# Branch product: three direct k tiles, four pairs by blocks, five direct, all sums on VectorE; MLP operand sums on VectorE; the bias of w2 added at its first accumulators

## The chip, the cores and the metric

The kernel runs on one core of a Trainium2 chip. The metric is the device time of one launch in microseconds, taken as the median of several runs.

## What is computed

One layer over 1024 latent tokens (x, width 1024) and 256 context tokens: two token mixers side by side (a Mamba-2 SSD branch and a gated linear recurrence), a gated merge, an output projection, and a squared-ReLU MLP. Everything is float32. Cut to what the change touches:

```
u      = gated_rmsnorm(y_ssd, z, ssd_norm_w)               # 1024 x 2048
br_ssd = u @ w_br_ssd                                      # 2048 x 1024: "the branch product"
x_mix  = (g_ssd * br_ssd + g_lru * br_lru) @ w_out
x      = layer_norm(alpha * x + mx[2] * x_mix, ln1_g, ln1_b)
h2     = layer_norm(x) * (1 + mx[4]) + mx[3]
mlp    = square(relu(h2 @ w_mlp1 + b_mlp1)) @ w_mlp2 + b_mlp2
out    = layer_norm(alpha * x + mx[5] * mlp, ln2_g, ln2_b)
```

## The kernel before

Every float32 operand is split into a high part (ScalarE copy, `A.activation(hi, raw, AF.Copy)`) and a low part (VectorE subtract), and every product is three matmuls on TensorE: high by high, high by low, low by high (`mm3`). A matmul here is 128 x 128 by 128 x 512.

**The branch product** has 16 k tiles of 128. Before, `wino` does them in two chunks of four pairs, by blocks in the manner of Strassen and Winograd: instead of eight block products there are seven (n = 1, 5, 6, 7, 2, 4, 3), each of 4 pairs x 4 output tiles x 3 matmuls = 48, so 2 x 7 x 48 = 672 matmuls, named `wp`. The operands of a block product are sums of input tiles (line L615: names `k0`, `k1`, `s1`), and the outputs are sums of products (L618, L659: name `ba`). `on=None` puts most of those sums on GpSimd (G, shown as POOL); the first sums of the first chunk, two of the output combinations and the additions of the second chunk run on VectorE (V, shown as DVE), which also makes every low part (`oll`, `orl`, L611). The inputs of u are scaled by a row of reciprocal norms (`rb`, loaded by a broadcast DMA) in a VectorE instruction (L710) of 128 x 1024.

**The merge** (`acc<-k,wh`) with the LRU branch and the **output projection** (`op`, L937 to L939) follow. For each of eight token tiles VectorE adds the projection to x (L940), normalises it (L132 to L826), and ScalarE makes `xn` (L821), which TensorE transposes (`tp`, L918). On the first token tile VectorE also scales the row of w2's bias by the gate (`rbmlp<-rbmlp,rmx`, L945, behind the DMA `rmx<-drow`), and GpSimd adds that row to each of the eight token tiles (L946) before the tile is stored.

**The first MLP product** works by blocks too, with operands T1 to T4 and B22 formed from the blocks of h2. The upper blocks are kept only as high and low parts, so GpSimd adds those up again (L974, L985, L986) and makes another difference (L987); VectorE makes L981, L983 and the low parts (L840). `others` issues the products in the order T2, T1, T4, T3, B22. The weight sums for each group are made by `prep` on GpSimd (L891 to L897).

**The second MLP product** (w2) already has the form that the branch gets now: direct k tiles in front, whose 16 output tiles ScalarE copies out of PSUM (L1111), four pairs by blocks per chunk with all sums on VectorE, and direct tiles behind.

All DMAs are issued by SP's queue in one order, and an instruction that waits holds up all behind it on its engine. The order on each engine comes from a scheduler that follows program order, priorities (`tc.high_priority`) and the reuse of pool buffers.

Of the kernel before, what the change touches and what calls it, by code (L numbers as in the profile page):

```python
# [60 lines left out]
def tile_hybrid_layer(ctx: ExitStack, tc: tile.TileContext, x, xc, wmod, win, wdt, lruw, wbs, wbl,  # L61
# [528 lines left out]
    def wino(kts, chunks, raw0, raw1, opr, load_l, load_r, accs, preset, fin, hook, add5, von=(), on=None, bank=0):  # L590
# [4 lines left out]
        for q, ch in enumerate(chunks):  # L595
# [50 lines left out]
            for ni, n in enumerate((1, 5, 6, 7, 2, 4, 3)):  # L646
# [8 lines left out]
                for i in range(4):  # L655
# [10 lines left out]
                    elif n == 7:  # L666
                        comb(3, a[7][i], a[7][i], a[6][i], OP.add)
                        comb(4, a[6][i], a[6][i], a[5][i], OP.add)
                        comb(5, a[5][i], fin5[i], a[7][i], OP.add)
                        fin(1, 1, i, a[5][i])  # L670
# [3 lines left out]
                if hook and last and n in (7, 3):  # L674
                    hook(n)

# [5 lines left out]
    kb0 = bx.enter_context(tc.tile_pool(name="kb0", bufs=8, side="right", reuse_waits="tile"))  # L682
    ac = bx.enter_context(tc.tile_pool(name="bac", bufs=12, side="right", reuse_waits="tile"))
    ox = ExitStack()
    kb1 = ox.enter_context(tc.tile_pool(name="kb1", bufs=2, side="right", reuse_waits="tile"))
# [5 lines left out]

    def braw1():
        n1[0] += 1
        if n1[0] % 8 in (1, 2):
            return kb1.tile([128, 1024], F32, name="k1", bufs=2)
        return wp.tile([128, 1024], F32, tag={3: "wr", 4: "wr", 5: "wh", 6: "wl", 7: "wh", 0: "wl"}[n1[0] % 8], name="k1", bufs=2)

    def load_bw(k, t_):
        Q.dma_start(t_, wbs[k])
        return t_  # L700
# [3 lines left out]
    def load_u(t, t_):  # L704
# [4 lines left out]
        Q.dma_start(t_, du[t])  # L709
        V.scalar_tensor_tensor(t_, t_, vec("normw", t), rbs[g], op0=OP.mult, op1=OP.mult)  # L710
        return t_

    accs = [[mhA.tile([128, 512], F32, tag={2: "mhh", 4: "mhh", 1: "mhl", 6: "mhl"}[n], name="ba", bufs=8) if n in (1, 6, 2, 4) else
             ac.tile([128, 512], F32, name="ba", bufs=12) for i in range(4)] for n in (1, 5, 6, 7, 2, 4, 3)]
# [29 lines left out]
    for th in range(2):  # L744
        sl = slice(th * 512, th * 512 + 512)
        yt = []
        with tc.high_priority(offset=100):
            for k in range(KT):
                raw = evp.tile([128, 512], F32, tag="ev", name="yraw")
                Q.dma_start(raw, dyl[k][:, sl])  # L750
                t_ = braw0().bitcast(F32R)
# [46 lines left out]
    b2r = brow(cp, "bmlp2")  # L798
# [122 lines left out]

    toks = []
    for th in range(2):
        tok = []
        for i in range(4):
# [37 lines left out]
    w0 = prep(0, None)  # L963
# [4 lines left out]
    rws = [cp.tile([128, 2, 512], F32, tag="r" + n_, name="rw", bufs=1) for n_ in ("ln1g", "ln1b", "bmlp2")]  # L968
    r12, r21, r22 = [], [], []
    sums = []  # L970
    b2t = wp.tile([128, 2, 512], F32, tag="wr", bufs=2, name="b2t")
    for k in range(KH):
        sums.append(tt.tile([128, 512], F32, name="b1", bufs=KH))
        G.tensor_tensor(sums[k], B11[k][0].bitcast(F32), B11[k][1].bitcast(F32), op=OP.add)  # L974
    with tc.high_priority(offset=2000):
        for k in range(KH):
# [8 lines left out]
            G.tensor_tensor(b11, B21[k][0].bitcast(F32), b11, op=OP.subtract)  # L985
            G.tensor_tensor(b11, b11, B21[k][1].bitcast(F32), op=OP.add)  # L986
            G.tensor_tensor(b12, b22, b12, op=OP.subtract)  # L987
            r12.append(b12)
            r21.append(b11)
            r22.append(b22)  # L990
        for dst, src in ((T4, r21), (T3, r12), (B22, r22)):
            for k in range(KH):
                split_to(dst[k], ALL, src[k])
# [102 lines left out]
    def direct(ops, i, n_, tag="acc", bufs=4):  # L1096
        pt = ps.tile([128, 512], F32, tag=tag, bufs=bufs, name="mo")
        ts_ = slice(i % 4 * 128, i % 4 * 128 + 128)
        for j, (la, rb) in enumerate(ops):
            mm3(pt, la[i // 4][0][:, ts_], la[i // 4][1][:, ts_], rb[n_][0], rb[n_][1], j == 0, j == len(ops) - 1)  # L1100
        return pt

    with tc.high_priority(offset=60):
        front = [halves(m, of_mha) for m in FRONT[:2]]
        front += [whole(m, raw1) for m in FRONT[2:]]
    pre = {}
# [100 lines left out]
```

## Time and profile before

| | |
|---|---|
| three runs | 2434.9, 2440.69, 2438.38 us, median 2438.38 |
| profiled run | 2443.13 us |
| its span, first to last instruction | 2441.3 us |
| TensorE busy | 96% |
| VectorE, ScalarE, GpSimd busy | 77%, 46%, 17% |
| mean granted clock of TensorE | 0.987 |

The profiled run is one execution. Matmuls are pipelined, so what TensorE loses is read from the starts of its matmuls and from how many of them lie in a stretch.

### The profile page before, as it was taken

Reading aid. Unit: us, or ns where it says so; the run is one execution under the profiler, and the core shown is the slowest. Engines: PE = TensorE matmul, PEld = TensorE weight load, DVE = VectorE, ACT = ScalarE, POOL = GpSimd, SP = SyncE. Lnnn points to the kernel's source line nnn. Section 1 sums busy time; section 2 is a strip of 40 time slices with the busy share of each in tenths; the row PEclk is TensorE's granted clock in tenths of the full one; section 3 lists DMA queues with packets and bytes.
Section 4 is the critical chain, followed back from the end, with each engine's and each line's share of the span. In section 5 each row is a group of like instructions: output and inputs, shape, how many; then the busy total and the mean of one; then the engine's idle time right before and its main releaser. Section 6 shows DMA issues by size and latency. Waiting matters only on the chain. (4 is left out here: it accounts for less than half of the span.)

```text
span 2441.3 us, 31541 instructions
## 1 busy us (share of the span) xinstructions
PE 2353.7 (96%) x11437; PEld 1877.2 (77%) x11437; DVE 1889.2 (77%) x3170; ACT 1112.5 (46%) x1947; POOL 418.3 (17%) x357
## 2 busy tenths in 40 slices
PE   7999999999999999999999998899979999999998
PEld 3877888787877878787787886577757888888876
DVE  6986688678888887888886579977687555638998
ACT  3766856544344354434434363232255554545421
POOL 1000000001011010101111346501365322000004
PEclk9999999999999999999999999999989999999999
DMA  9422144323334253433325640367225333614132
GB/s 345 133 65 66 57 163 154 97 77 105 87 96 112 70 139 77 114 87 96 105 78 142 229 156 26 106 219 244 87 73 164 112 114 100 257 70 149 59 112 87
DMA packets 131636, 294.73 MB, mean 121 GB/s; under 512 B 14596, under 2 KB 47492, under 8 KB 131352
## 3 DMA queue, kind: packets, MB, share of 16 engines
q1 hardware_dynamic: 131480, 292.71, 37.7%
q8 instruction: 90, 1.47, 0.3%
q14 instruction: 66, 0.54, 0.1%
HBM read 243.83 MB, written 53.03 MB: 122 GB/s over the span
## 5 line engine op out<-in xcount | busy, mean ns | idle before, releaser
L114 PE MATMUL acc<-hl,wh 128*128 128x512 f32 (+1 forms) x1560 | 595.9, 382 | 0.6 <-DVE hl L182 0.6
L115 PE MATMUL acc<-hh,wl 128*128 128x512 f32 (+1 forms) x1560 | 593.8, 381 | 0.0
L113 PE MATMUL acc<-hh,wh 128*128 128x512 f32 (+1 forms) x1560 | 591.0, 379 | 2.2 <-ACT hh L177 2.2
L114 PEld LDWEIGHTS acc<-hl,wh 128*128 128x128 f32 x1560 | 295.3, 189 | 58.1 <-issue 12.9
L113 PEld LDWEIGHTS acc<-hh,wh 128*128 128x128 f32 x1560 | 295.1, 189 | 51.8 <-issue 3.1
L115 PEld LDWEIGHTS acc<-hh,wl 128*128 128x128 f32 x1560 | 295.2, 189 | 47.8 <-issue 4.5
L544 POOL TENSOR_SCALAR_AFFINE_SELECT R<-R 128x512 f32<-128x512 f32 x128 | 93.4, 753 | 1114.8 <-DMA R<-dcum 1094.3
L114 PE MATMUL wp<-orl,olh 128*128 128x512 f32 x504 | 201.0, 399 | 23.7 <-DVE orl L611 23.7
L549 ACT ACTIVATE L<-R,cumT 128x128 f32<-128x128 f32 x512 | 163.5, 390 | 126.4 <-issue 58.1
L102 ACT ACTIVATE wh<-wr 128x1024 fp32r<-128x1024 f32 x113 | 119.4, 1057 | 221.4 <-PE acc L114 157.5
L115 PE MATMUL wp<-orh,oll 128*128 128x512 f32 x504 | 198.3, 393 | 0.0
L113 PE MATMUL wp<-orh,olh 128*128 128x512 f32 x504 | 195.6, 393 | 0.3 <-DVE ba L659 0.2
L103 DVE TENSOR_TENSOR wl<-wr,wh 128x1024 fp32r<-128x1024 f32 x113 | 140.3, 1242 | 28.7 <-ACT wh L102 26.7
L114 PEld LDWEIGHTS wp<-orl,olh 128*128 128x128 f32 x504 | 95.5, 189 | 52.3 <-DVE orl L611 32.7
L527 DVE SCALAR_TENSOR_TENSOR H<-H,dec,misc 128x64 f32<-128x64 f32 x512 | 104.9, 274 | 24.1 <-PE misc L519 23.1
L97 POOL TENSOR_TENSOR mv<-mv,mhalf 128x1 f32<-128x1 f32 x34 | 30.5, 898 | 526.1 <-DVE mv L96 524.3
L610 ACT ACTIVATE olh<-k 128x512 fp32r<-128x512 f32 x108 | 67.9, 629 | 109.1 <-PE wp L114 107.2
L113 PEld LDWEIGHTS wp<-orh,olh 128*128 128x128 f32 x504 | 95.7, 190 | 21.6 <-DVE ba L659 0.6
L115 PEld LDWEIGHTS wp<-orh,oll 128*128 128x128 f32 x504 | 95.9, 190 | 19.3
L611 DVE TENSOR_TENSOR oll<-k,olh 128x512 fp32r<-128x512 f32 x108 | 88.0, 815 | 28.2 <-ACT olh L610 27.9
L611 DVE TENSOR_TENSOR orl<-k,orh 128x512 fp32r<-128x512 f32 x126 | 104.5, 830 | 1.6 <-ACT orh L610 1.6
L888 DVE TENSOR_TENSOR xl<-wr,xh 128x512 fp32r<-128x512 f32 x75 | 74.7, 1000 | 32.2 <-ACT xh L887 31.9
(325 smaller groups left out, 4982.0 us busy)
## 6 DMA issues: line engine op xcount, KB each, us to landing
wr<-in_win_dram SPq DMA_DIRECT2D x80, 512.0 KB, 3.6
R<-dcum SPq DMA_DIRECT2D x64, 512.0 KB, 5.2
wr<-in_w_dram SPq DMA_DIRECT2D x37, 512.0 KB, 3.8
wm<-in_wmod_dram SPq DMA_DIRECT2D x32, 512.0 KB, 3.7
E<-decum SPq DMA_DIRECT2D x64, 256.0 KB, 4.5
da<-r SPq DMA_DIRECT2D x64, 256.0 KB, 2.8
k<-da SPq DMA_DIRECT2D x26, 512.0 KB, 5.7
k<-in_w_dram SPq DMA_DIRECT2D x20, 512.0 KB, 4.7
```

What stands on the lines that cost most here:

```text
L97: G.tensor_tensor(dst, dst, mhalf[:, :n], op=OP.pow)
L102: A.activation(hi, src, AF.Copy)
L103: V.tensor_tensor(lo, src, hi.bitcast(F32), op=OP.subtract)
L113: P.matmul(pt, wh, mh, start=first, stop=False)
L114: P.matmul(pt, wh, ml, start=False, stop=False)
L115: P.matmul(pt, wl, mh, start=False, stop=last)
L527: V.scalar_tensor_tensor(H[:, k, d_, hs_2], H[:, k - 1, d_, hs_2], dec[:, k, d_ * 32 + 2 * t + h:d_ * 32 + 2 * t + h + 1], sp[:, k - k0, d ...
L544: G.affine_select(out=rv, in_=rv, compare_op=OP.is_ge, fill=-BIG, base=0, pattern=[[0, 2], [0, 2], [sg, 128]], channel_multiplier=-sg)
L549: A.activation(L[:, q], R[:, q, (p % 2) * 128:(p % 2 + 1) * 128], AF.Exp, bias=ncumT[:, p, col:col + 1])
L610: A.activation(hi, src, AF.Copy)
L611: V.tensor_tensor(lo, src, hi.bitcast(F32), op=OP.subtract)
L888: V.tensor_tensor(ts[i][1], v, ts[i][0].bitcast(F32), op=OP.subtract)
```

## The change

- Branch product: k tiles 0 to 2 go directly (`direct`: 16 output tiles x 3 tiles x 3 matmuls = 144 matmuls, copied out of PSUM by ScalarE), tiles 3 to 10 as four pairs by blocks (336 matmuls, all sums on VectorE), tiles 11 and 12 directly (96 matmuls), tiles 13 to 15 directly (144). The output tiles of the direct parts behind are added by VectorE (L786 after). Together 720 matmuls.
- `rb` has one buffer in place of two.
- The blocks of h2 are also written to DRAM (`dh2`, eight stores) and read back (`b1`, `b21`, eight loads); the sums of the T operands and the first `prep` run on VectorE. `others` takes T1, T2, T3, T4, B22 with T4 formed from a reloaded tile.
- L945, the DMA `rmx` and the eight L946 are gone. The bias of w2 is loaded into the buffer of `ln2g` and added by VectorE at the evacuation of w2's front tiles; `ln2g` itself is loaded again later.

```diff
-    wino([c_ * 8 + k + h_ for c_ in range(2) for k in range(4) for h_ in (0, 4)], [4, 4], braw0, braw1, bop,
-         load_bw, load_u, accs, (), bfin, None, None, (2,3))
+    with tc.high_priority(offset=HP0):
+        front = [parts(t, of_kbf, in_ac, 2, 1) for t in range(3)]
+    pre = {}
+    for r_, c_ in ((0, 0), (1, 0), (0, 1), (1, 1)):
+        pre[r_, c_] = [ac.tile([128, 512], F32, name="ba", bufs=16) for i in range(4)]
+        for i in range(4):
+            A.activation(pre[r_, c_][i], direct(front, r_ * 4 + i, c_), AF.Copy)
+    def bhook(n):
+        if n == 6:
+            btail[0] = [parts(t, of_kbf, in_evp, 2, 1) for t in range(11, 13)]
+        elif n == 3:
+            btail[1] = [parts(13, of_kbf, braw0, 1, 1)] + [parts(t, of_bop, braw0, 1, 2) for t in range(14, 16)]
+    wino([k + h_ for k in range(3, 7) for h_ in (0, 4)], [4], braw0, braw1, bop,
+         load_bw, load_u, accs, (2, 3, 4), bfin, bhook, badd5, on=V, bank=1)
+    for q in range(2):
+        for c_ in range(2):
+            for i in range(8):
+                pt = direct(btail[q], i, c_, *(("acc", 4), ("y", 3))[q])
+                V.tensor_tensor(ys[i][c_], ys[i][c_], pt, op=OP.add)
...
-            rbs[g] = kb1.tile([128, 1024], F32, name="rb", bufs=2)
+            rbs[g] = kbf.tile([128, 1024], F32, name="rb", bufs=1)
...
-            if th == 0 and i == 0:
-                V.scalar_tensor_tensor(b2r, b2r, 1.0 / ALPHA, brow(cp, "mx5", "x1", NX), op0=OP.mult, op1=OP.mult)
-            G.tensor_tensor(xt, xt, b2r, op=OP.add)
...
+                Q.dma_start(dh2[k], hf)
...
-    w0 = prep(0, None)
+    w0 = prep(0, None, on=V)
...
-        G.tensor_tensor(sums[k], B11[k][0].bitcast(F32), B11[k][1].bitcast(F32), op=OP.add)
+        Q.dma_start(sums[k], dh2[k])
+    for k in range(KH):
+        r21s.append(evp.tile([128, 512], F32, tag="ev", name="b21"))
+        Q.dma_start(r21s[k], dh2[KH + k])
...
-            A.activation(t_, direct(front, r_ * 4 + i, c_), AF.Copy)
+            V.tensor_tensor(t_, ln2g[:, c_ * 512:c_ * 512 + 512], direct(front, r_ * 4 + i, c_), op=OP.add)
```

**At the end of the branch product**, VectorE's order before: low parts of the last block products (`oll`, `orl`) between additions of products from PSUM (`wp`) into `ba`.

```order
L611 TENSOR_TENSOR oll_13464<-k0_13074,olh_13463 128x512
L611 TENSOR_TENSOR orl_13468<-k0_13076,orh_13467 128x512
L618 TENSOR_TENSOR ba_12336<-ba_12336,ba_12328 128x512
L659 TENSOR_TENSOR ba_12337<-ba_12337,wp_13309 128x512
L611 TENSOR_TENSOR oll_13504<-k1_13079,olh_13503 128x512
L611 TENSOR_TENSOR orl_13508<-k1_13081,orh_13507 128x512
L618 TENSOR_TENSOR ba_12337<-ba_12337,ba_12329 128x512
L659 TENSOR_TENSOR ba_12338<-ba_12338,wp_13310 128x512
```

After the change, the same place: the last evacuations of the block products, then the operands of direct tiles 12 to 15 (`kf`, `tl`; L723 is the scaling by `rb`), and only then the first additions of direct output tiles (`mo`, L786).

```order
L659 TENSOR_TENSOR ba<-ba,wp 128x512 x2
L618 TENSOR_TENSOR ba<-ba 128x512 x2
L737 TENSOR_TENSOR kf<-k_13389,kf 128x1024
L737 TENSOR_TENSOR tl<-k_13396,th 128x512 x2
L723 SCALAR_TENSOR_TENSOR k_13406<-k_13406,vt,rb 128x1024
L737 TENSOR_TENSOR tl<-k_13419,th 128x512 x2
L737 TENSOR_TENSOR tl<-k_13406,th 128x512 x2
L723 SCALAR_TENSOR_TENSOR k_13429<-k_13429,vt,rb 128x1024
L786 TENSOR_TENSOR ba<-ba,mo 128x512 x2
L737 TENSOR_TENSOR tl<-k_13429,th 128x512 x2
L786 TENSOR_TENSOR ba<-ba,mo 128x512 x5
```

Nothing of the direct tiles stood on VectorE here before; now nine operand instructions (some rows hold two, x2) stand between the last block evacuation and the first `mo` addition, and two of them (L723) read the `rb` row of the last group.

**Between the first two token tiles of the output projection**, VectorE before:

```order
L820 SCALAR_TENSOR_TENSOR mv<-mv 128x1
L945 SCALAR_TENSOR_TENSOR rbmlp_14638<-rbmlp_14638,rmx_14759 128x1024
L940 SCALAR_TENSOR_TENSOR x_14764<-x_14764,op 128x512 x2
L132 BN_STATS st_14818<-x_14764 128x6 x2
L134 BN_AGGR mv<-st_14818 128x2
```

And after (L882 and L1001 are the lines L820 and L940 of before):

```order
L882 SCALAR_TENSOR_TENSOR mv<-mv 128x1
L1001 SCALAR_TENSOR_TENSOR x_14727<-x_14727,op 128x512 x2
L132 BN_STATS st_14781<-x_14727 128x6 x2
L134 BN_AGGR mv<-st_14781 128x2
L96 TENSOR_SCALAR mv<-mv 128x1
```

The addition of the projection now stands directly behind the statistics of the tile before.

**Where the T operands of the MLP are formed**, VectorE before (`b` is a T operand, `rw` and `b2t` are blocks of h2, `tl` and `mhl` low parts):

```order
L981 TENSOR_TENSOR b_15639<-rw,b_15639 128x512
L981 TENSOR_TENSOR b_15641<-rw,b_15641 128x512
L840 TENSOR_TENSOR tl<-b_15639,th 128x512
L983 TENSOR_TENSOR b_15639<-rw,b_15639 128x512
L981 TENSOR_TENSOR b_15643<-rw,b_15643 128x512
```

And after:

```order
L1043 TENSOR_TENSOR b_15603<-rw,b_15603 128x512
L959 TENSOR_TENSOR wr<-wr 128x512
L1043 TENSOR_TENSOR b_15605<-rw,b_15605 128x512
L902 TENSOR_TENSOR tl<-b_15603,th 128x512
L1050 TENSOR_TENSOR rw<-rw 128x512
L1045 TENSOR_TENSOR b_15603<-rw,b_15603 128x512
```

VectorE's queue has gained the last weight sum (L959) and the differences of `rw` (L1050), which stood on GpSimd before (L897 and L987).

## Rows read from the trace of the kernel before

**Rows 1.** Cores: span and mean granted clock.
```profile
core 0: 2441.3 us, clock 0.987
```

**Rows 2.** Windows: length; busy (count) PE, PEld, DVE, ACT, POOL; clock; DMA; GB/s.
```profile
1385.70:1569.80 184.10, 162.99 (x674) 128.06 (x674) 164.74 (x163) 81.28 (x143) 113.45 (x69) 0.97 0.27 89
...
1690.00:1712.00 22.00, 17.42 (x68) 13.86 (x67) 16.57 (x29) 2.49 (x2) 8.88 (x6) 0.84 0.45 173
...
1765.00:1793.00 28.00, 20.67 (x93) 16.10 (x92) 17.37 (x25) 11.01 (x15) 15.74 (x11) 0.98 0.33 112
1793.00:1843.00 50.00, 39.09 (x147) 28.77 (x148) 45.38 (x45) 27.70 (x47) 30.59 (x20) 0.84 0.24 80
...
2106.00:2165.00 59.00, 58.27 (x256) 47.62 (x255) 29.79 (x45) 27.00 (x46) 0.00 (x0) 1.00 0.43 164
```

**Rows 3.** Windows again: a stretch of w2's block products.
```profile
2170.00:2300.00 130.00, 130.00 (x575) 107.55 (x574) 110.07 (x178) 64.89 (x112) 0.00 (x0) 1.00 0.26 92
```

**Rows 4.** Waits, 1386 to 1570: us in total, times, longest.
```profile
POOL k L615 <- DVE oll L611: 40.3, 6, 19.5
...
PE wp L114 <- DVE orl L611: 20.8, 15, 3.2
```

**Rows 5.** Timeline of VectorE, 1384 to 1408: start, duration.
```profile
1402.62 1.76 DVE L611 TENSOR_TENSOR orl<-k,orh 128x512 fp32r<-128x512 f32 x1
...
1406.00 0.68 DVE L611 TENSOR_TENSOR oll<-s,olh 128x512 fp32r<-128x512 f32 x1
1406.60 0.68 DVE L611 TENSOR_TENSOR orl<-k,orh 128x512 fp32r<-128x512 f32 x1
```

**Rows 6.** Timeline of GpSimd, 1388 to 1408.
```profile
1403.80 1.73 POOL L615 TENSOR_TENSOR k<-k,k 128x512 f32<-128x512 f32 x1
```

**Rows 7.** VectorE's lines by shape, 2165 to 2345: count, busy, mean ns, idle before.
```profile
L611 DVE TENSOR_TENSOR orl<-k,orh 128x512 fp32r<-128x512 f32 x62 | 42.4, 683 | 0.0
...
L659 DVE TENSOR_TENSOR ma<-ma,wp 128x512 f32<-128x512 f32 x38 | 24.7, 678 | 0.0
...
L1055 DVE TENSOR_TENSOR k<-k,k 128x1024 fp32r<-128x1024 f32 x8 | 9.5, 1217 | 1.3 <-ACT k L1054 1.3
```

**Rows 8.** Timeline of TensorE, 1545 to 1548.
```profile
1544.59 0.50 PE L114 MATMUL wp<-orl,olh 128*128 128x512 f32 x1 [3.23 <-DVE orl L611]
...
1546.54 0.63 PE L115 MATMUL wp<-orh,oll 128*128 128x512 f32 x1
1546.96 0.63 PE L113 MATMUL wp<-orh,olh 128*128 128x512 f32 x1
```

**Rows 9.** DMA issues, 1380 to 1600: KB each, median us to landing.
```profile
k<-du SPq DMA_DIRECT2D x9, 512.0 KB, 5.3
```

**Rows 10.** Waits, 1690 to 1712.
```profile
PE op L937 <- DVE x L940: 4.6, 1, 4.6
...
DVE rbmlp L945 <- DMA rmx<-drow: 1.9, 1, 1.9
```

**Rows 11.** Timeline of VectorE, 1690 to 1712.
```profile
1694.65 0.16 DVE L820 SCALAR_TENSOR_TENSOR mv<-mv 128x1 f32<-128x1 f32 x1 [0.68 <-POOL mv L97]
1696.71 1.23 DVE L945 SCALAR_TENSOR_TENSOR rbmlp<-rbmlp,rmx 128x1024 f32<-128x1024 f32 x1 [1.89 <-DMA rmx<-drow]
1697.94 1.29 DVE L940 SCALAR_TENSOR_TENSOR x<-x,op 128x512 f32<-128x512 f32 x2
```

**Rows 12.** Waits, 1765 to 1793.
```profile
PE tp L918 <- ACT xn L821: 6.5, 2, 5.4
```

**Rows 13.** Waits, 1793 to 1843.
```profile
PE pd L113 <- ACT th L839: 5.7, 2, 3.8
...
PE pd L115 <- DVE xl L888: 2.5, 2, 1.9
...
PE pd L114 <- DVE tl L840: 2.2, 2, 1.8
```

**Rows 14.** ScalarE's lines by shape, 2106 to 2165.
```profile
L1111 ACT ACTIVATE ma<-mo 128x512 f32<-128x512 f32 x16 | 9.2, 597 | 23.7 <-PE mo L115 23.7
```

More of the change, by code (lines that the diff above doesn't have):

```diff
@@ L673, in wino, with direct @@
                         fin(*{2: (0, 0), 4: (1, 0), 3: (0, 1)}[n], i, a[n][i])
-                if hook and last and n in (7, 3):
+                if hook and last:
                     hook(n)
+    def direct(ops, i, n_, tag="acc", bufs=4):
+        pt = ps.tile([128, 512], F32, tag=tag, bufs=bufs, name="mo")
+        ts_ = slice(i % 4 * 128, i % 4 * 128 + 128)
+        for j, (la, rb) in enumerate(ops):
+            mm3(pt, la[i // 4][0][:, ts_], la[i // 4][1][:, ts_], rb[n_][0], rb[n_][1], j == 0, j == len(ops) - 1)
+        return pt
+    FULL = slice(0, 1024)
     a2.close()
@@ L713, in tile_hybrid_layer, with parts @@
-    accs = [[mhA.tile([128, 512], F32, tag={2: "mhh", 4: "mhh", 1: "mhl", 6: "mhl"}[n], name="ba", bufs=8) if n in (1, 6, 2, 4) else
-             ac.tile([128, 512], F32, name="ba", bufs=12) for i in range(4)] for n in (1, 5, 6, 7, 2, 4, 3)]
+        Q.dma_start(t_, du[t][:, sl])
+        V.scalar_tensor_tensor(t_, t_, vec("normw", t), rbs[g][:, sl], op0=OP.mult, op1=OP.mult)
+        return t_
+    def parts(t, get, tmp, nr, nd):
+        o_ = []
+        for q, ld in enumerate((load_bw, load_u)):
+            raws = [ld(t, tmp(), slice(j * 1024 // nr, (j + 1) * 1024 // nr)) for j in range(nr)]
+            raws = [r[:, j:j + 512] for r in raws for j in range(0, 1024 // nr, 512)] if nd == 2 else raws
+            dst = [get(q) for _ in range(nd)]
+            for j, raw in enumerate(raws):
+                (hi, lo), n = dst[j * nd // len(raws)], 1024 // len(raws)
+                sl = slice(j * n % (1024 // nd), j * n % (1024 // nd) + n)
+                A.activation(hi[:, sl], raw, AF.Copy)
+                V.tensor_tensor(lo[:, sl], raw, hi[:, sl].bitcast(F32), op=OP.subtract)
+            o_.append([(hi[:, j:j + 512], lo[:, j:j + 512]) for hi, lo in dst for j in range(0, 1024 // nd, 512)])
+        return o_
@@ new lines, in of_kbf, with of_bop, in_evp, in_ac @@
+    def of_kbf(q):
+        return [brawf().bitcast(F32R) for _ in "hl"]
+    def of_bop(q):
+        return [bop.tile([128, 512], F32R, tag="o" + "lr"[q] + c, name="t" + c, bufs=NOP) for c in "hl"]
+    def in_evp():
+        return evp.tile([128, 512], F32, tag="ev", name="bt")
+    def in_ac():
+        return ac.tile([128, 512], F32, name="ba", bufs=16)
+    with tc.high_priority(offset=HP0):
[5 more added lines that the diff above has]
+            A.activation(pre[r_, c_][i], direct(front, r_ * 4 + i, c_), AF.Copy)
@@ L715, in tile_hybrid_layer @@
+    accs = [pre[{2: (0, 0), 4: (1, 0), 3: (0, 1)}[n]] if n in (2, 4, 3) else
+            [mhA.tile([128, 512], F32, tag={1: "mhl", 6: "mhl", 5: "mhh", 7: "mhh"}[n], name="ba", bufs=8) for i in range(4)]
+            for n in (1, 5, 6, 7, 2, 4, 3)]
     ys = [[None, None] for _ in range(8)]
@@ L920, in h2_tile @@
         return hf
+    dh2 = [dr.tile([128, 512], F32, name=f"dh{k}") for k in range(KT)]
     toks = []
@@ L967, in tile_hybrid_layer @@
     T1, T2, T4 = ([block_tiles(tb, "t", 12) for k in range(KH)] for _ in range(3))
-    rws = [cp.tile([128, 2, 512], F32, tag="r" + n_, name="rw", bufs=1) for n_ in ("ln1g", "ln1b", "bmlp2")]
-    r12, r21, r22 = [], [], []
-    sums = []
+    rws = [cp.tile([128, 2, 512], F32, tag=n_, name="rw", bufs=b_) for n_, b_ in (("rln1g", 1), ("rln1b", 1), ("rbmlp2", 1))]
+    r12, r22 = [], []
+    sums, r21s = [], []
     b2t = wp.tile([128, 2, 512], F32, tag="wr", bufs=2, name="b2t")
@@ L984, in tile_hybrid_layer @@
             split_to(T2[k], ALL, b11)
-            G.tensor_tensor(b11, B21[k][0].bitcast(F32), b11, op=OP.subtract)
-            G.tensor_tensor(b11, b11, B21[k][1].bitcast(F32), op=OP.add)
-            G.tensor_tensor(b12, b22, b12, op=OP.subtract)
             r12.append(b12)
-            r21.append(b11)
             r22.append(b22)
-        for dst, src in ((T4, r21), (T3, r12), (B22, r22)):
-            for k in range(KH):
-                split_to(dst[k], ALL, src[k])
+        for k in range(KH):
+            V.tensor_tensor(r12[k], r22[k], r12[k], op=OP.subtract)
+            split_to(T3[k], ALL, r12[k])
+        for k in range(KH):
+            V.tensor_tensor(r21s[k], r21s[k], sums[k], op=OP.subtract)
+            split_to(T4[k], ALL, r21s[k])
+        for k in range(KH):
+            split_to(B22[k], ALL, r22[k])
     tx.close()
@@ L1094, in of_k1 @@
         return get
[L1096 to L1101, printed above, removed]
     with tc.high_priority(offset=60):
@@ L1135, in hook @@
             tail[0] = [whole(m, tail_raw) for m in TAIL[0]]
-        else:
+        elif n == 3:
             gate.append(raw1())
```

54 lines of the change are left out of this document (27 added, 27 removed).

## Prediction, made before the changed kernel ran

> **What bounds the kernel now.** The profiled execution took 2443.1 us with a span of 2441.3 [rows 1]; its own time lies 4.7 us above the median of the three runs, 2438.4, so a sum made against it is moved down by 4.7 at the end. TensorE is the bound nearly everywhere, so the question is what it loses, and where. I read the windows first: in the block products of w2, with nothing on GpSimd, 575 matmuls lie in 130.00 us, 0.226 us each, which I take as the undisturbed step [rows 3]. Held against that step, four stretches lose time [rows 2]. The branch product: 184.1 us for 674 matmuls that need 152.4, so 31.7 lost. The first token tiles of the output projection (1690 to 1712): 22.0 for 68, so 6.6 lost. The end of the projection and the transposes (1765 to 1793): 28.0 for 93, so 7.0. The T operands (1793 to 1843): 50.0 for 147, so 16.8. In the last two the count holds some short transposes, so the loss is a little larger. What ends the waits is next. In the branch it is VectorE's low parts, 20.8 us in 15 waits [rows 4], and the reader should see in the timeline why VectorE is late: the same instruction takes 1.76 us while GpSimd runs a sum of 1.73 and 0.68 when GpSimd is idle [rows 5, 6]. [...]
>
> [...]
>
> **The change, part by part.**
>
> Branch product, TensorE: 720 matmuls for 672, 48 x 0.226 = +10.9 us of work. If nothing waited, the stretch would take 722 x 0.226 = 163.2 in place of 184.1: a gain of 20.9 is the most it can give.
>
> Branch product, VectorE: it takes over GpSimd's sums. With GpSimd idle its rows take 0.68 of record, but begin 0.60 apart (1406.00, 1406.60) [rows 5]; 128 x 1024 takes 1.22 [rows 7]. The order has 132 rows from the first sum that needs the last pair's weights to the last operand ahead of the first addition of a direct output tile, six of them 128 x 1024: 126 x 0.61 + 6 x 1.22 = 84.2 us. When can they begin? That load goes into a buffer that the direct front frees, and TensorE ends its 144 front matmuls at 1386.0 + 32.6 = 1418.6 (the first k tile some 1.5 us sooner); a load of its size lands in 5.3 [rows 9]: about 1422.5. So VectorE reaches the first addition at 1506.7 and has it done at 1507.4 (0.68 for a PSUM source [rows 7]). TensorE ends the seven block products at 1386.0 + 480 x 0.226 = 1494.5, fills four accumulators of the direct tiles (24 matmuls, to 1500.0), and the order gives it 19 matmuls of the last part (4.3, to 1504.3): it waits 3.1 us. I add 3.4 for some steps at the low clock (10 matmuls cost 2.0 more) and for short waits on operands, since VectorE runs only some 2 us ahead of each product. Loss 6.5, gain 20.9 - 6.5 = **14.4**. Nearest likeness: w2's block products, all on VectorE, lose nothing over 130 us with VectorE busy 110 [rows 3]. Bounds: 20.9; and 2, by the second rival. ScalarE's 16 front copies are 0.60 each [rows 14] and lie beside a front in which it has only splits to do.
>
> Bias row: L940 could have gone at 1694.8, when L820 ended, but L945 stood ahead of it, waiting 1.9 for its row, and it went at 1697.9; TensorE waited 4.6 for it [rows 10, 11]. Without L945 L940 goes 3.1 sooner and a wait of 1.5 stays. With that the low clock (0.84 in this window [rows 2]) should mostly vanish, worth up to 1.9. Gain **4** (3.1 to 5.0). The eight L946 go too; their cost is in the next part.
>
> End of projection and T operands: together 23.8 lost [rows 2]. The waits: the transposes for the last token tiles' `xn`, 6.5 [rows 12], then the products for T operands, 10.4 [rows 13]. Before, GpSimd's sums sat in the same queue as the root (L97) of the normalisation and doubled VectorE's rows. After, the normalisation's root has GpSimd to itself. What comes in its place: VectorE must do 36 rows (16 sums and differences, 20 low parts, by the order) at 0.61 = 22.0 us, while the five products they feed are 60 matmuls, 13.6 us. So 8.4 may stay, if VectorE has no lead. Gain 23.8 - 8.4 = **15.4**. Bounds: 23.8; and 7, if the reload of h2 is late (third rival). The eight stores and eight loads of 256 KB ride on DMA engines that are 0.24 to 0.33 busy there [rows 2]; what they can delay is SP's queue, where the last token tile of x stands behind two of the reloads. Its cover is some 73 matmuls of the MLP's first products (16.5 us) against a load of about 5.
>
> w2's front: 16 evacuations of 0.60 on ScalarE become 16 additions of 0.68 on VectorE [rows 7, 14], 10.8 us more on an engine busy 29.8 of 59 [rows 2]; they stand in order among low parts, and the first waits for the bias row. I cost it at **-1** (0 to -4).
>
> Everything else keeps its order. Sum: 14.4 + 4 + 15.4 - 1 = 32.8, so 2410.3 for an execution like the profiled one, and 2410.3 - 4.7 = **2406** against the median.
>
> **The rivals.**
>
> All waits go: 20.9 + 5.0 + 23.8 = 49.7, 2389. For it: w2's blocks [rows 3]. Against: the in-order rows ahead of the first addition.
>
> VectorE's step is its record's length. If rows begin 0.68 apart and not 0.60, the 126 rows take 10 us longer, the first addition comes at 1517, TensorE waits 13 there and runs at the low level for a while (2 to 3): the branch gains about 2, the whole 20.4, 2418. For it: rows on VectorE that wait on one another, as sums in place do, might not overlap; in the free stretch only independent rows are seen at 0.60 [rows 5]. Against: w2's blocks hold the same dependent sums [rows 3, 7].
>
> [...]
>
> The reload is late: T4's source waits in SP's queue behind weights and stores. Then T4, the fourth product, holds TensorE and the start of the MLP gains 7 in place of 15.4: sum 24.4, 2414.
>
> Slower: VectorE is a step behind at every operand, and the short waits keep TensorE at its low level. A matmul then costs 0.43 - 0.226 = 0.20 more [rows 8]; it takes 165 of the 336 block matmuls at that level to eat 32.8, and all of them (+67) would end 34 above, 2472. For it: with one `rb` buffer each group's row is loaded only when the last scaling with it is done, four times 5.3 plus 1.3 before the blocks run, and everything waits in one order. Against: before, 15 waits in this stretch left the clock at 0.97 [rows 2, 4], so short waits do not pull it down. Just past the point, 2445.
>
> **How the numbers follow.** Forecast (2397 to 2415) 0.43; second rival 0.19; late reload 0.14; all waits gone 0.12; slower, or a gain eaten by such waits, 0.12. The first four lie between 2389 and 2418; the range goes on to 2428, where the low bounds of all parts add up (2 + 3.1 + 7 - 4 = 8, so 2430), and down to 2387. A measurement here tells about 0.2% (5 us) from no change. Of the last case I put 0.08 above 2443 and 0.04 within; a sum of low bounds is at the border of it, so faster 0.87, same 0.05, slower 0.08.
>
> **What would show it.** In the changed profile: VectorE rows of 0.68 and an empty GpSimd through the branch; the branch in 167 to 172 us from first front matmul to merge; one wait of TensorE on VectorE's additions (`ba`) at the first direct tile behind the blocks, about 3 us; between the first two token tiles a wait near 1.5; transposes with no wait over 3; T operand waits below 8.4 in all. The prediction is wrong if block products start late one after another (`orl` or `olh` waits at each), if the reload `b21` is what T4 waits for, or if the front of w2 waits for its bias row.

## The result and the profile after

The changed kernel takes 2410.74 us (median of four runs, 2407.9 to 2412.37) beside 2439.53 for the kernel before on the same chip (four runs, 2434.9 to 2443.19). The ratio is 0.9881 with a 95% interval of 0.9863 to 0.9898: 1.2% faster. The forecast was 2406.0 with a range of 2387 to 2428. The two profiled executions took 2443.13 and 2411.09 us, 32.0 apart; the forecast sum was 32.8.

The span and clock of the profiled run answer to [rows 1]; the busy times of the engines stand under them. GpSimd's share fell from 17% to 10%, TensorE's rose from 96% to 98%.

```profile
core 0: 2409.3 us, clock 0.991
```

```profile
PE 2351.3 (98%) x11485; PEld 1881.1 (78%) x11485; DVE 1841.8 (76%) x3240; ACT 1094.0 (45%) x1909; POOL 243.5 (10%) x253
```

**Where the 32 us came from.** The stages are separated by landmarks on TensorE's timeline: the first matmul of the merge, the last of the output projection, the last of the first MLP product. Before (start, duration, line, operation):

```profile
1569.99 0.40 PE L113 MATMUL acc<-k,wh 128*128 128x512 f32 x1
...
1768.22 0.40 PE L939 MATMUL op<-oh,mhl 128*128 128x512 f32 x1
...
2106.21 0.40 PE L115 MATMUL pd<-mhh,xl 128*128 128x512 f32 x1
```

After:

```profile
1553.63 0.39 PE L114 MATMUL acc<-kf,wh 128*128 128x512 f32 x1
...
1748.66 0.40 PE L1000 MATMUL op<-oh,mhl 128*128 128x512 f32 x1
...
2070.57 0.40 PE L115 MATMUL pd<-mhh,xl 128*128 128x512 f32 x1
```

| stage | lead at its end | its own share | predicted |
|---|---|---|---|
| branch product | 1569.99 - 1553.63 = 16.4 | +16.4 | +14.4 |
| merge and projection | 1768.22 - 1748.66 = 19.6 | +3.2 | +4 |
| first MLP product | 2106.21 - 2070.57 = 35.6 | +16.0 | +15.4 |
| w2 to the end | 2441.3 - 2409.3 = 32.0 | -3.6 | -1 |

Seven matmuls of the first MLP product stood ahead of the last projection matmul before, and none after. So 1.6 of the 3.2 (7 x 0.226) only moved across a landmark: without that shift the merge and projection gained 1.6 and the first MLP product 17.6.

The sizes agree better than the reasons do, as the next views show. First the windows that answer to [rows 2]: the branch, the first token tiles, w2's front, and the end of the projection with the T operands in two pieces, each shifted to the same work.

```profile
core 0: us, PE busy (x) PEld busy (x) DVE busy (x) ACT busy (x) POOL busy (x), PEclk, DMA share, GB/s
1385.64:1553.63 167.99, 164.96 (x723) 134.91 (x722) 136.60 (x208) 66.81 (x117) 0.00 (x0) 1.00 0.36 124
1672.00:1694.00 22.00, 16.98 (x69) 13.62 (x68) 14.98 (x29) 3.34 (x4) 2.79 (x4) 0.92 0.37 131
2070.00:2129.00 59.00, 56.76 (x241) 45.51 (x240) 38.43 (x58) 14.04 (x21) 0.00 (x0) 0.97 0.44 166
...
1745.40:1773.40 28.00, 27.83 (x137) 22.55 (x136) 23.99 (x41) 17.98 (x26) 2.93 (x3) 1.00 0.50 169
1773.40:1823.40 50.00, 44.69 (x181) 35.03 (x181) 42.96 (x58) 31.45 (x54) 17.26 (x12) 0.93 0.48 153
```

With the step of 0.226 us: the branch loses 167.99 - 723 x 0.226 = 4.6 (31.7 before, 6.5 predicted); the first token tiles 22.0 - 69 x 0.226 = 6.4 (6.6 before, 2.6 expected); the end of the projection with the T operands 78.0 - 318 x 0.226 = 6.1 (23.8 before, 8.4 predicted); w2's front 59.0 - 241 x 0.226 = 4.5 (59.0 - 256 x 0.226 = 1.1 before). So the branch and the T operands did what was forecast, the wait at the bias row's place stayed, and w2's front lost more.

**The branch.** VectorE's timeline: the first sum that needs the last pair's weights, two rows a little later, and the first addition of a direct output tile (L786).

```profile
1423.36 0.69 DVE L615 TENSOR_TENSOR s<-k,kf 128x512 f32<-128x512 f32 x1 [4.44 <-DMA kf<-in_wbs_dram]
...
1427.10 0.68 DVE L615 TENSOR_TENSOR k<-s,k 128x512 f32<-128x512 f32 x1
1427.70 0.68 DVE L615 TENSOR_TENSOR k<-k,k 128x512 f32<-128x512 f32 x1
...
1507.56 1.27 DVE L786 TENSOR_TENSOR ba<-ba,mo 128x512 f32<-128x512 f32 x2
```

The row sum of the forecast was 1422.5 + 84.2 = 1506.7; the engine took 1507.56 - 1423.36 = 84.2, with one wait of 0.7 in it. Rows start 0.60 apart although their records are 0.68 long. TensorE's waits at that place, 1495 to 1555, are these (us in total, times, longest):

```profile
PE mo L113 <- ACT th L736: 1.8, 2, 1.0
PE mo L114 <- DVE kf L737: 0.8, 1, 0.8
...
```

2.8 us in all with a third of 0.2 on `tl`, close to the 3.1 expected, but none of it is for an addition (`ba`): TensorE waits for the operands of the tail tiles, one step ahead of the additions in VectorE's order.

**Between the first two token tiles** (all engines' waits from 1672, then VectorE and SP there) the answer to [rows 10, 11] is:

```profile
PE op L998 <- DVE x L1001: 5.0, 1, 5.0
DVE x L1001 <- DMA x<-in_x_dram: 4.2, 2, 2.1
```

```profile
1680.10 1.28 DVE L1001 SCALAR_TENSOR_TENSOR x<-x,op 128x512 f32<-128x512 f32 x2 [2.02 <-DMA x<-in_x_dram]
```

```profile
1675.53 0.33 SPq L1005 DMA_DIRECT2D dx<-x  x1
1675.95 0.38 SPq L992 DMA_DIRECT2D x<-in_x_dram  x1
```

L945 is gone, and L1001 still starts 2.18 us after the last statistic of the tile before (L882 at 1677.92; before, 3.29 from L820 to L940). What it waits for now is the x tile itself. SP issues that load (L992) behind the store of the first token tile (L1005), which leaves at 1675.53, when VectorE has just written that tile (L888, to 1675.49). The queue had issued nothing since 1669.68. Before, the same load stood ahead of that store and left 12.1 us earlier than it:

```profile
1688.38 0.46 SPq L931 DMA_DIRECT2D x<-in_x_dram  x1
1700.46 0.33 SPq L947 DMA_DIRECT2D dx<-x  x1
```

**At the T operands** TensorE's waits from 1745 to 1820 answer to [rows 12, 13]:

```profile
PE pd L115 <- DVE xl L950: 2.2, 1, 2.2
PE pd L113 <- ACT th L901: 1.8, 1, 1.8
PE pd L114 <- DVE tl L902: 1.3, 1, 1.3
```

```profile
1785.93 0.68 DVE L902 TENSOR_TENSOR mhl<-b2t,mhh 128x512 fp32r<-128x512 f32 x1
...
1791.94 0.69 DVE L1053 TENSOR_TENSOR b<-b,b 128x512 f32<-128x512 f32 x1 [4.13 <-DMA b<-dh]
1793.33 1.80 DVE L902 TENSOR_TENSOR tl<-b,th 128x512 fp32r<-128x512 f32 x1
```

```profile
1763.42 15.69 SPq L914 DMA_DIRECT2D da<-r  x2
...
1788.00 0.33 SPq L1036 DMA_DIRECT2D b<-dh  x1
```

5.3 us of waits are left of 16.9, and the transposes, which had 6.5 of them, wait 0.2. VectorE (second fence) does not lag: by 1788 it has nothing left but T4, and then stands idle for 4.13 until T4's source is back. That reload leaves at 1788.00, in SP's order behind stores (third fence, first row: two issues that reach from 1763.42 to 1779.11) and two weight loads (L938, from 1781.22). Once it is there, the first low part of T4 (1793.33) is 1.80 long beside GpSimd's next `prep`, whose four sums reach from 1793.31 to 1799.63; the next one, at 1800.10, is 0.68 again.

**At w2's front**, 2066 to 2094, TensorE waits for ScalarE, and ScalarE for the load of one of the front's own weight tiles:

```profile
ACT k L1117 <- DMA k<-dw: 3.4, 2, 2.8
...
PE mo L113 <- ACT k L1117: 2.2, 1, 2.2
```

### The profile page after: what moved, and what is told of

Its sections match the earlier page's. It is cut to its first block, busy times and chain, and to the rows that moved or that the text cites. A ratio compares the mean times of both kernels' runs of the same rounds, so it can differ in the third digit from the quotient of the medians.

```text
span 2409.3 us, 31481 instructions
## 1 busy us (share of the span) xinstructions
PE 2351.3 (98%) x11485; PEld 1881.1 (78%) x11485; DVE 1841.8 (76%) x3240; ACT 1094.0 (45%) x1909; POOL 243.5 (10%) x253
## 4 chain that ended last, share of the span: by engine, by line
PE 77%; DVE 11%; DMA 6%; ACT 3%; issue 2%; POOL 0%; SPq 0%; POOLq 0%; DVEq 0%; ACTq 0%
PE acc L114 11%; PE acc L115 11%; PE acc L113 11%; PE pd L115 4%; PE pd L113 4%; PE pd L114 4%; PE wp L114 3%; PE wp L115 3%; PE wp L113 3%; PE mo L114 3%; PE mo L115 3%; PE mo L113 3%; PE misc L519 2%; PE y L558 2%; PE y L556 1%
## 5 line engine op out<-in xcount | busy, mean ns | idle before, releaser
L114 PE MATMUL wp<-orl,olh 128*128 128x512 f32 x392 | 153.1, 391 | 2.1 <-DVE orl L611 2.1
L115 PE MATMUL wp<-orh,oll 128*128 128x512 f32 x392 | 152.6, 389 | 0.0
L113 PE MATMUL wp<-orh,olh 128*128 128x512 f32 x392 | 149.9, 390 | 0.3 <-DVE ba L659 0.3
L97 POOL TENSOR_TENSOR mv<-mv,mhalf 128x1 f32<-128x1 f32 x34 | 29.7, 874 | 789.2 <-DVE mv L96 778.7
L234 DVE SCALAR_TENSOR_TENSOR xf<-acc,cw,xf 128x504 f32<-128x504 f32 (+1 forms) x96 | 62.4, 650 | 37.3 <-ACT xf L228 35.6
L610 ACT ACTIVATE olh<-k 128x512 fp32r<-128x512 f32 x81 | 51.1, 631 | 86.1 <-PE wp L114 81.2
L114 PEld LDWEIGHTS wp<-orl,olh 128*128 128x128 f32 x392 | 73.6, 188 | 18.8 <-DVE orl L611 3.8
L113 PEld LDWEIGHTS wp<-orh,olh 128*128 128x128 f32 x392 | 74.0, 189 | 16.3 <-DVE ba L659 0.7
L950 DVE TENSOR_TENSOR xl<-wr,xh 128x512 fp32r<-128x512 f32 x75 | 67.3, 900 | 24.3 <-ACT xh L949 24.1
L115 PEld LDWEIGHTS wp<-orh,oll 128*128 128x128 f32 x392 | 73.6, 188 | 15.2
L519 PEld LDWEIGHTS misc<-xs,bt 128*128 128x128 f32 x576 | 77.1, 191 | 9.8 <-DVE xs L512 3.0
```

The costliest lines, as they stand in the source:

```text
L113: P.matmul(pt, wh, mh, start=first, stop=False)
L114: P.matmul(pt, wh, ml, start=False, stop=False)
L115: P.matmul(pt, wl, mh, start=False, stop=last)
L234: V.scalar_tensor_tensor(dv[:, :, sh:], pv[:, :, :L - sh], w[k], dv[:, :, sh:], op0=OP.mult, op1=OP.add)
L519: P.matmul(sp[:, k - k0, d_], bt[:, KD[k]], xs[:, d_, KD[k] - min(KD[k0:k0 + n])], start=True, stop=True)
L610: A.activation(hi, src, AF.Copy)
```

## The experiments

Each kernel ran beside the kernel before on the same chip, whose median was 2439.4 to 2439.6 in every batch. "Behind" and "ahead" below compare landmarks with those of the changed kernel above. A landmark is read from one profiled execution. In the changed kernel and runs 1, 2, 3, 6, 7 and 8, whose branch is the same, the branch takes 166.3 to 168.7 us from its first matmul to the merge, so a difference of some 2 us in one stage between two kernels can be scatter.

**1. The x load ahead.** Theory: the second token tile waits for its x, because the load stands behind a store in SP's queue. One more tile is loaded early.

```diff
-    x0 = [cp.tile([128, 1024], F32, name="x1", bufs=NX) for _ in range(1)]
+    x0 = [cp.tile([128, 1024], F32, name="x1", bufs=NX) for _ in range(2)]
...
```

> Changed kernel, with the second token tile of x loaded ahead like the first, so that its load no longer stands behind the store of the first normalised tile in SP's queue. My theory: the wait that L945 caused was replaced by this load (it was issued at 1675.95, right behind the store that VectorE's last step on the first tile released, and landed 4 us later); so TensorE's wait of 5.0 us there falls to 1 to 2 us and the time to about 2406 (ratio to before 0.986). Rival: the chain of VectorE's statistics is the limit and the load was only the last to come; then a wait of 3 us or more stays and the time is 2409 or above.

2409.53 us (2408.36 to 2411.7), ratio 0.9882 (0.9867 to 0.9896). TensorE's waits from 1660 to 1700:

```profile
PE tp L978 <- ACT xn L883: 3.2, 1, 3.2
PE op L998 <- DVE x L1001: 2.2, 1, 2.2
```

The 5.0 at the second tile is gone, so the load was its cause; 2.2 comes back at the third tile and 3.2 at the transposes. The time does not differ from that of the changed kernel.

**2. The bias row on another queue.** Theory: w2's front waits because the bias row's load joins a burst in SP's queue. The row goes into ln2b's buffer, on ScalarE's queue and earlier.

```diff
+    with tc.high_priority(offset=400):
+        A.dma_start(ln2b, _ap(rows, ROWS["bmlp2"] * 1024, [[0, 128], [1, 1024]]))
...
-    Q.dma_start(ln2g, _ap(rows, ROWS["bmlp2"] * 1024, [[0, 128], [1, 1024]]))
...
```

> Changed kernel, with the row of w2's bias loaded into the other norm row's buffer by ScalarE's queue, ahead of the rush of loads for w2's front, in place of SP's queue in the middle of it. My theory: the front of w2 lost 7.3 us (3.3 before) because half a megabyte of bias row went ahead of the copied weight tile that the third front tile needs (landed 5.7 us after issue, 3.9 before); without it the wait of 2.2 us on ScalarE's copy goes, the low clock behind it too, and the time falls by 3 to 4 to about 2407. Rival: the sixteen additions on VectorE in place of ScalarE copies delay the operand rows; then the front still loses 6 or more and the time stays at 2411.

2410.41 (2409.23 to 2412.6), ratio 0.9886 (0.987 to 0.9903). The wait at the front is still there:

```profile
PE mo L113 <- ACT k L1117: 2.4, 1, 2.4
```

The theory fell: the bias row is not what the front waits for.

**3. The bias as before.** The scaled row, its DMA, the eight additions on GpSimd and ScalarE's plain evacuations come back; the rest stays changed.

```diff
...
+            if th == 0 and i == 0:
+                V.scalar_tensor_tensor(b2r, b2r, 1.0 / ALPHA, brow(cp, "mx5", "x1", NX), op0=OP.mult, op1=OP.mult)
+            G.tensor_tensor(xt, xt, b2r, op=OP.add)
...
-            V.tensor_tensor(t_, ln2g[:, c_ * 512:c_ * 512 + 512], direct(front, r_ * 4 + i, c_), op=OP.add)
+            A.activation(t_, direct(front, r_ * 4 + i, c_), AF.Copy)
...
```

> Changed kernel with the bias of w2 put back as before: scaled by VectorE behind its DMA (L945's step), added by GpSimd to each of the eight token tiles, and the front of w2 copied out by ScalarE. My theory from the two traces: the bias part of the change gained nothing in the projection (5.0 us of wait for 4.6) and lost 4 in w2's front, so putting it back makes the kernel 2 to 4 us faster, 2407 to 2409, unless GpSimd's eight additions again slow the normalisation of the last token tiles. Rival, my prediction's sum: the bias part was worth 3 us, so 2414, and the waits of the last transposes come back.

2416.61 (2411.37 to 2418.04), ratio 0.9906 (0.9891 to 0.9921): the bias part is worth about 5.9 us (one of the four runs, 2411.37, lies among those of the changed kernel), where the theory expected the kernel to get faster. It is not at the place where I looked for it. The last projection matmul starts at 1749.55, 0.9 behind, the last of the first MLP product at 2077.51, 6.9 behind. Some 15 matmuls of that product (3.4 us) stand ahead of the first of these landmarks here and none in the changed kernel, so the product itself loses about 9.4. The waits of TensorE from 1745 to 1820:

```profile
PE pd L113 <- ACT xh L952: 4.3, 1, 4.3
PE pd L113 <- ACT wh L952: 2.6, 2, 2.0
```

The part lengthens the way to the MLP's weight operands (`xh`, `wh`). The longest of these waits goes back to a weight load that ScalarE waits for, and SP's queue held that load for a low part on VectorE:

```profile
ACT xh L952 <- DMA wr<-in_w_dram: 7.6, 1, 7.6
SPq L941 <- DVE mhl L905: 7.5, 1, 7.5
```

That low part (of `b2t`) starts at 1796.63, and at 1785.93 in the changed kernel; the load leaves right behind it, at 1797.37. What makes VectorE later was not taken apart. The additions of the row (L1010, 2.39 us on GpSimd) hold two stores in SP's queue for 9.7 us in this stretch; they do not hold up the root of the normalisation (L97), which waited for VectorE's statistics there. At w2's front 2.5 of wait stays even with ScalarE's copies, so the additions on VectorE are not its cause either.

**4. The branch's sums back on GpSimd.** The changed kernel in its new form, with the sums placed much as before.

```diff
-         load_bw, load_u, accs, (2, 3, 4), bfin, bhook, badd5, on=V, bank=1)
+         load_bw, load_u, accs, (2, 3, 4), bfin, bhook, badd5, (2, 3), bank=1)
```

> Changed kernel with the sums of the branch's blocks put back on GpSimd as before, the form of 3 direct, 4 pairs, 5 direct kept. My theory: what the branch gained is VectorE freed of GpSimd, so its rows go back to 1.7 us beside GpSimd's sums, TensorE waits 15 to 25 us more and the time is 2426 to 2436. Rival: the direct tiles in front and behind are the gain, since they give VectorE time to run ahead; then the branch stays within 5 us of 168 and the time within 2411 to 2416.

2438.57 (ten runs, 2435.3 to 2443.76), ratio 0.9997 (0.9988 to 1.0007): the whole gain is gone, and a little more than the theory said (2426 to 2436). The branch's window, TensorE's waits in it, and two rows of VectorE beside one of GpSimd:

```profile
1385.00:1580.00 195.00, 173.02 (x722) 138.30 (x721) 144.59 (x164) 65.26 (x117) 74.71 (x44) 0.96 0.31 107
```

```profile
PE wp L114 <- DVE orl L611: 12.6, 7, 4.2
PE mo L113 <- DVE ba L786: 7.6, 1, 7.6
```

```profile
1434.75 1.78 DVE L611 TENSOR_TENSOR oll<-s,olh 128x512 fp32r<-128x512 f32 x1
1436.45 0.68 DVE L611 TENSOR_TENSOR orl<-k,orh 128x512 fp32r<-128x512 f32 x1
```

```profile
1434.24 1.73 POOL L615 TENSOR_TENSOR k<-kf,k 128x512 f32<-128x512 f32 x1
```

The same low part is 1.78 long while GpSimd's sum runs and 0.68 right after it, as in [rows 5, 6]. The merge starts at 1580.18, 26.6 behind, and the gap at the end of the span is 29.6. Against the kernel before, the merge starts 10.2 later: with its sums on GpSimd the new form pays for its 48 more matmuls (10.9) as well, and the stages behind it only make up for that (2.4 ahead at the span's end).

In these rows 0.68 grows by 1.10 beside a sum of 1.73, and the low part ends 0.56 after the sum does (1436.53 and 1435.97).

**5. The kernel before, with only its branch sums on VectorE.** This keeps the two chunks of four pairs and has no direct tiles.

```diff
-         load_bw, load_u, accs, (), bfin, None, None, (2,3))
+         load_bw, load_u, accs, (), bfin, None, None, on=V)
```

> Kernel before, with one edit: all sums of the branch's two chunks of four pairs on VectorE, no direct tiles, 672 matmuls. VectorE's work in the stretch is then about 232 rows, 150 us at 0.61 and 1.22, against 152 us of matmuls. My theory: GpSimd's interference is most of what the branch lost, but with VectorE this full TensorE still waits some 8 to 18 us, so the branch takes 160 to 172 (184 before) and the time is 2415 to 2427. Rival: without GpSimd nothing waits, the direct tiles were not needed and their 10.9 us are a loss; then the branch takes 157 or less and the time is below 2413. Other rival: VectorE becomes the bound; branch 178 or more, time 2433 or more.

2414.87 (2413.01 to 2417.04), ratio 0.99 (0.9884 to 0.9917). One argument gives 24.5 of the 28.8 us. The branch:

```profile
1385.20:1538.90 153.70, 153.32 (x673) 125.90 (x672) 136.69 (x215) 79.37 (x140) 0.00 (x0) 1.00 0.27 94
```

673 matmuls in 153.70 us, 0.228 each: apart from one wait of 0.3 nothing waits, though VectorE is busy for 136.69 of them. That is 14.3 us shorter than the new form (167.99), so the direct tiles are not what removes the waits; they cost 48 matmuls (10.9) and the 2.8 of waits at the tail. This is the first rival's branch (157 or less), though the time did not fall below its 2413: of the 31.1 us by which the merge starts earlier than before, 29.6 are left at the end of the profiled span.

**6. The MLP operands as before.** The sums and differences of h2's blocks and the first `prep` go back to GpSimd, the stores and reloads of h2 and the new order of products go. Theory: the 17 us gained at the start of the MLP came from VectorE's rows no longer running beside GpSimd's sums, so 10 to 17 come back, less 4 at w2's front: 2417 to 2424.

```diff
-    w0 = prep(0, None, on=V)
+    w0 = prep(0, None)
...
-        Q.dma_start(sums[k], dh2[k])
...
+        G.tensor_tensor(sums[k], B11[k][0].bitcast(F32), B11[k][1].bitcast(F32), op=OP.add)
...
```

> Changed kernel with the MLP operands put back as before: no copy of h2 in DRAM, the sums of the T operands and the first weight sums on GpSimd, products in the order T2, T1, T4, T3, B22. [...] Rival: the eight additions L946 alone were the trouble (putting them back cost 6), and the T sums on GpSimd cost no more than 5: 2407 to 2414.

2420.19 (2417.02 to 2424.39), ratio 0.9921 (0.9906 to 0.9935): 9.5 slower than the changed kernel. The last matmul of the first MLP product starts 10.4 behind (2080.99). The waits of TensorE from 1745 to 1820:

```profile
PE pd L113 <- ACT th L901: 4.8, 1, 4.8
PE pd L115 <- DVE wl L950: 2.4, 1, 2.4
PE tp L980 <- ACT xn L883: 2.3, 1, 2.3
```

Two of them, for `th` and `xn`, are waits of [rows 12, 13] again, smaller (5.7 and 6.5 before). Runs 3 and 6 both lose in the first MLP product, about 9.4 and 10.0, beside the 17.6 that the change gained there (each with the shift across the landmark counted in). So both parts of the change have a share in it, and the shares overlap or scatter by some 2 us.

**7. The old order of products.** From the second pair of output blocks on, `others` takes T2, T1, T4, T3, B22 again. Theory: the new order moves the last stores between the loads of w2's front.

```diff
+        if p == 0:
...
+            return
+        p6 = prod(w[0], T2)
+        u2 = plus(xa, p6, md, "xu")
         p5 = prod(w[1], T1, "y", 3)
-        u2 = plus(xa, prod(w[0], T2), md, "xu")
...
+        p4 = prod(w[2], T4, "y", 3)
...
```

> Changed kernel with the order of the MLP's products as before (T2, T1, T4, T3, B22) for all groups but the first; the sums stay on VectorE. The bias row moved off SP's queue did not help the front of w2, nor did ScalarE's copies in the run with the bias as before: both still waited 2.4 for the copied weight tile. New theory: the new order ends each group later on the side of its stores, so SP's queue holds the loads of the second pair and of the copied weight tile behind the last store; with the old order those loads stand ahead of it. The front's loss falls from 7.3 to about 3.3, the time by 3 to 4, to 2407. Rival: the front's loss comes from somewhere else, or the MLP's groups lose by the old order what the front wins: 2410 to 2412 again.

2408.97 (2408.04 to 2411.43), ratio 0.9875 (0.986 to 0.989). The wait of 2.2 at the front is gone. TensorE's longest wait from 2060 to 2100 is now:

```profile
PE wp L113 <- ACT orh L610: 0.8, 1, 0.8
```

From the last matmul of the first MLP product to the end it now takes 2408.1 - 2071.18 = 336.9 in place of 338.7 (335.1 before). All kernels here agree on that: with the new order this stretch takes 338.1 to 339.6 (the changed kernel and runs 1, 2, 3, 4 and 9), with the old order in the changed kernel 336.8 to 336.9 (runs 6, 7, 8 and 10), and 335.1 and 335.9 in the kernel before and run 5. So the order explains 1.8 of w2's 3.6. The first MLP product takes 323.1 in place of 321.9, which is within the scatter, and the time does not tell the two kernels apart.

**8. The old order and three x tiles ahead.** Both mended together.

> The run before this, and the first three token tiles of x loaded ahead. With two loaded ahead the wait of 5.0 at the second tile went, but a wait of 2.2 came at the third, whose load stood behind the second store, and one of 3.2 on the transposes of the first tiles. My theory: with three the wait at the third goes too, and the window of the first token tiles loses 2 to 4 in place of 7.4; with the front's 3.5 the time is 2403 to 2405. Rival: the transposes wait for the normalisation in any case and the T operands after them take up what is won, as they did with two; 2407 or above.

2410.39 (2406.97 to 2411.64), ratio 0.9877 (0.9862 to 0.9892): no gain. TensorE's longest wait from 1660 to 1760 shows where x's gain went:

```profile
PE tp L989 <- ACT xn L883: 7.2, 3, 4.8
```

Its waits at the projection are down to 0.2. With x there in time TensorE reaches the transposes earlier and waits for `xn`, the end of the normalisation, which did not become faster.

**9. Two chunks on VectorE, with the other two parts of the change.** The branch's form of run 5, in the changed kernel. The branch's code of before comes back with it: no direct tiles, its pools, `rb` with two buffers.

```diff
...
-    wino([k + h_ for k in range(3, 7) for h_ in (0, 4)], [4], braw0, braw1, bop,
-         load_bw, load_u, accs, (2, 3, 4), bfin, bhook, badd5, on=V, bank=1)
+    wino([c_ * 8 + k + h_ for c_ in range(2) for k in range(4) for h_ in (0, 4)], [4, 4], braw0, braw1, bop,
+         load_bw, load_u, accs, (), bfin, None, None, on=V)
...
```

> Changed kernel with one thing different: the branch product in its form of before (two chunks of four pairs, 672 matmuls, no direct tiles), with all sums on VectorE. In the kernel before with its sums on VectorE that stretch took 153.5 us from first product to merge, against 168.0 in the changed kernel. My theory: the direct tiles are a cost, 10.9 us of matmuls and 4 of waits, so the time falls by 12 to 15, to 2396 to 2399 (ratio to before 0.982 to 0.984). Rival: a branch that ends earlier only meets the next limit, the weights of the merge (a wait of 2.9 on ScalarE's copy was new in that run) and the output projection's loads, and 5 or less arrives at the end: 2405 to 2411.

2401.91 (2400.92 to 2406.27), ratio 0.985 (0.9837 to 0.9864): the fastest kernel here, 37.6 us below the one before. The time lies between the theory (2396 to 2399) and the rival (2405 to 2411). The merge starts at 1539.48, 14.2 ahead of the changed kernel, but the last projection matmul (1736.55) is 12.1 ahead, the last of the first MLP product (2060.63) 9.9, and the span's end 9.9. TensorE's largest waits between 1540 and 1830 are these:

```profile
PE pd L113 <- ACT xh L884: 5.6, 1, 5.6
PE op L933 <- DVE x L936: 5.6, 1, 5.6
PE acc L113 <- ACT wh L102: 2.6, 1, 2.6
```

**10. The same with the old order of products.**

> The run before this, and the MLP's products in the order of before for all groups but the first. My theory: the two gains add, as they lie in different stretches: 1 to 3 us less than the run before this, 2394 to 2397. Rival: no difference from it beyond 1 us.

2401.93 (2401.61 to 2405.6), ratio 0.9849 (0.9835 to 0.9862): no difference from run 9. From 2062.70 to the end is 336.8 in place of 338.8, and the first MLP product takes 2062.70 - 1737.14 = 325.6 in place of 324.1.

## Why the prediction was right, and which steps were not

**The main mechanism held.** The branch lost its time to low parts that came late while GpSimd summed. Putting the sums back on GpSimd (run 4) costs 27.8 us, and taking them off GpSimd in the kernel before gains 24.5 (run 5). What the runs do not separate is how much of it is the lengthening of VectorE's rows and how much GpSimd's own slower sums (1.29 to 2.36 us each in run 4 from 1428 to 1436, beside 0.68 on VectorE).

**VectorE's step of 0.61 held**, and the rival that took its record's 0.68 as the rate fell: 84.2 us between the two marked rows, as worked out. The branch gained more than 14.4, because 4.6 and not 6.5 were lost: 168.0 us from its first matmul to the merge in place of 184.0 (1569.99 - 1386.00); the other 0.4 of the 16.4 were there when it began. w2, the nearest likeness in the forecast, runs five pairs per chunk (`chunks = [5, 5]`), not four as said ahead of the prediction; the rows read from it do not hang on that.

**"It waits 3.1 us" for the additions of the first direct tile** was right in size and wrong in what is waited for: 2.8 us, on the tail tiles' operands, which stand ahead of those additions in the order. Of the short waits for which I added the rest of the 6.5, 0.3 us came ahead of the tail. No run shows the ten matmuls at the low clock (2.0 of the 3.4): they were my estimate from the steps of 0.43 behind a wait of 3.23 [rows 8], where the granted clock before was 0.50 (1546.5 to 1547.5). In the branches of the changed kernel and of run 5, with all sums on VectorE, it was 1.00.

**"Without L945 L940 goes 3.1 sooner and a wait of 1.5 stays" failed.** The wait is 5.0. I took away one waiting instruction and did not ask when the next operand arrives: x stands in SP's queue behind a store, and the wait at a tile goes when its x is loaded ahead (runs 1 and 8). That the stage from merge to projection still gained 3.2 beside the 4 predicted is luck: 1.6 of it are the seven matmuls that moved across the landmark, and the longest gap between two matmul starts in the merge, at its operands, went from 4.34 to 2.72, which I had not counted. The bias part is nevertheless worth 5.9 (run 3), at the start of the MLP, where I had priced it only as part of another term.

**"8.4 may stay, if VectorE has no lead" had nearly the right size, 15.4 beside 16.0 (17.6 without the shift), for a wrong reason.** VectorE had the lead. The 5.3 that stayed come from T4's reload and from weights beside GpSimd's `prep`. So the mechanism of the late-reload rival, which the prediction also named as a sign of being wrong, did occur, with 4.13 us of idle on VectorE, but not at its price of 8.4: TensorE waited 1.8 and 1.3 for T4's parts. T4 is the fourth of the five products; the three ahead of it covered most of the lateness.

**w2's front at -1 was too small: the stage lost 3.6.** Of the two causes I named, the bias row's load (run 2) and the additions on VectorE (run 3) both fell. 1.8 of it is the order of the products ahead, a part of the change that the forecast put at nothing (run 7). The other 1.8 stay open.

**The form of the branch is itself a cost.** I priced the direct tiles as 10.9 us of work and did not ask what the old form would do with its sums on VectorE. It loses next to nothing in the branch (waits of 0.3 and 0.7 in runs 5 and 9), and kernel 9 is 8.8 us faster than the changed one.

**A gain in one stage did not come whole to the end.** 14.2 us won in the branch become 9.9 at the end (run 9), and the 5.0 of wait on x that run 1 takes away come back as 2.2 and 3.2, at the next tile and at the end of the normalisation.

**The sum's 0.8 is in part luck.** It compares two single executions, 32.0 us apart, while the medians are 28.8 apart. The forecast took 4.7 off on the way to the median, because the profiled run of before lay that much above the median of three runs; the profiled run of after lay only 0.4 above its own, and so the result is 4.7 higher than 2406.0. Within the sum, the terms of the branch and the T operands were too small, and those of the projection and of w2 too favourable.

## What to carry to other kernels

Where VectorE rows of one shape show two lengths (0.68 and 1.78 in run 4), put GpSimd's timeline beside them and try all sums on VectorE in the existing form before building a new form: here one argument gave 24.5 of 28.8 us, and the new form cost 14 of it again in the branch (8.8 in the time). When an instruction that waits is removed, look up what the next one on that engine needs and behind what its load stands in the queue. Follow a gain by landmarks from stage to stage to the end of the span: in run 9 the stages behind the branch took back 4.2 of 14.2.

## What the runs showed of the hardware

VectorE carried more than its record lengths say: 215 rows kept it busy for 136.7 of 153.7 us with one wait of TensorE (0.3, run 5), and neighbouring 128 x 512 rows started 0.60 apart with records of 0.68 (the changed kernel, 1427.10 and 1427.70 above). In run 4, from 1428 to 1437, rows of that shape were 1.66 to 1.78 long while GpSimd ran a sum and 0.68 right after, and GpSimd's sums took 1.61 to 2.36 beside VectorE's rows and 1.29 while VectorE stood idle, so moving work to GpSimd made both engines' rows longer there. And in the changed kernel a store that waited for its tile in SP's queue (nothing was issued from 1669.68 to 1675.53) held up a load behind it, for which SP shows no wait of its own, by which TensorE stood for 5.0 us while the DMA engines were busy 0.37 of that window (1672 to 1694).
